# Expert selection of tokens 128 to 255 moved behind the places of the fetched tokens, and the first four row buffers put into the mixer's columns

## The chip, the cores and the metric

The kernel runs on one core of a Trainium2 chip. The core has five engines that run their own instruction streams in order and wait for each other through semaphores: TensorE (PE, matrix products; PEld is its weight load), VectorE (DVE), ScalarE (ACT), GpSimd (POOL) and SyncE (SP, which here only issues transfers). Transfers between HBM and the on-chip memory (SBUF) are carried out by 16 DMA engines, whoever issues them. The metric is the device time of one execution in microseconds (us). "Before" stands at a median of 1466.97 us over three runs, 1466.46 to 1468.75.

## The reference, cut to what matters

The model has two layers over 256 tokens of 1024 features. Layer 0 mixes the tokens by attention and retention, layer 1 by a short convolution; each is followed by the same channel mixer, PEER, which is where the change is:

```python
q  = (t @ w_q).reshape(n_tok, 8, 2, 128)              # 8 heads, two halves
sc = einsum('thpd,hpnd->thpn', q, sub_keys)           # 128 scores per head and half
s1, i1 = top_k(sc[:, :, 0], 16);  s2, i2 = top_k(sc[:, :, 1], 16)
top_s, pos = top_k(all sums s1 + s2, 16)              # 16 of 16 x 16 candidates
eidx = (i1 * 128 + i2) taken at pos;  gate = softmax(top_s)
hid  = gelu(einsum('td,thkd->thk', t, u[eidx]))
out  = einsum('thk,thkd->td', gate * hid, v[eidx])
```

Each token picks 8 x 16 = 128 of 16384 experts, and an expert is a row of `u` and a row of `v`.

## The kernel before

**Two ways to an expert.** The first 96 tokens (TG) fetch the rows of their own experts. One step of a class `Gather` is an indirect DMA on POOL's queue (line 997) that brings 128 rows of 1024 numbers (512 KB), one for each partition, and a DVE instruction that uses them: for `u` a product summed along the row (L1007), for `v` a scaled addition (L1018). A layer has 96 steps for `u` and 96 for `v`. The other 160 tokens (TD) go through all experts densely: TensorE multiplies them with each of 128 blocks of `u` (`dense_u`, L1400) and then of `v`, and the weights of the experts that a token did not pick are zero. The zeros and gates are laid out by 40 groups of four tokens (`onehots` on DVE, `g_mm` on TensorE, `g_put`).

**The stages of a PEER layer.** First the projection: for f = 0 to 15 TensorE computes the queries of one head half (`u_tile`, L302 with the high part of the weights, then L308 with the low part) and the scores of the half before (L1129, copied out by ACT at L1132). Then "u": a loop over i = 0 to 127, one block of `u` each. Then "v", likewise. The two parts of a projection weight come from `_split` (L177 on ACT for the high part, L179 for the low part, on POOL for all weights but f = 1 and 2); `u_tile(f)` writes the split of weight f + 2 into the program before it does its own products.

**What sets the order.** The order of the instructions of each engine is that of the program text. DVE's selection work is cut into pieces that stand in a queue `Pump`: each piece has a price, each turn of the loop adds credit (3.2 per f, 1.4 per i), and pieces are written out while the credit lasts. The pieces are: `stage1(th, f)` (the top 16 of the scores of one head half for token half th, that is tokens 0 to 127 or 128 to 255: five instructions, L1116 to L1124, shown as eight), and `chain(th, hf)` for four heads (`stage2_build`, L1146 to L1154; `stage2_top`, L1116 to L1124 on the candidates; `extract`, L1201 to L1223). `places(hf)` then makes the row numbers of the fetched tokens (L1255, L1256) and puts them into the tile `IG`, partly by three DMAs on POOL's queue (L1248), partly by a DVE copy (L1249). Only token half 0 holds fetched tokens. When the queue is empty, the groups start: `onehots`, and from then on DVE multiplies each block's result (L1443).

**Row buffers.** The fetched rows land in two buffers `grow` and four buffers in the tile `x2`, which is the mixer's and the projection's normalised input and is free once the projection's last high product has read it. `ga.widen()` takes over `x2` after the projection; `issue()` asks for rows as long as a buffer is free, the places are known (32 steps after `places(0)`, all 96 after `places(1)`) and `ga.open` is set, which happens at i == 2. Until then `grow` holds two blocks of `u` brought early (`PRE`, fetched by `fetch(i)` on SP's queue, L1104, among other spare places: `hg`, `uhi`, `ulo`, `xb`, `ko`, and the tile `one`, which with one `ulo` tile holds block 58). `ga.step()` writes a row's consumption into the program at a given rate per i; after each consumption `issue()` asks for the next row. The remaining blocks of `u` stream through a ring of eight tiles (`raw`, L153 on SP).

`extract` uses two scratch areas: M1 and M2 lie over the scores SC[0][0] and SC[1][0], whose selection has ended by then.

Of the kernel before, what the change touches and what calls it, by code (L numbers as in the profile page):

```python
# [12 lines left out]
F16 = mybir.dt.float16  # L13
# [214 lines left out]
def trunk_kernel(ctx, tc, x, xn, cst, mcst, ew_in, ew_out, ow_in, ow_out, wq, keys, pu, pe_, pv, pvn, pun, gains, out):  # L228
# [731 lines left out]
    class Gather:  # L960
# [8 lines left out]
        def __init__(self, pool):  # L969
            few = pool.tile([P, ROWS, D], F32, tag="grow", name=nm("grow"))  # L970
            self.rows = [few[:, i, :] for i in range(ROWS)]
            self.acc = [pool.tile([P, D], F32, tag=f"gacc{q}", name=nm("gacc")) for q in range(3)]
            self.hid = pool.tile([P, STEPS], F32, tag="ghid", name=nm("ghid"))
            self.known = 0
            self.open = False
            self.rate = 0.0
            self.i = 0
            self.c = 0
            self.credit = 0.0
            self.later = {}  # L980

        def widen(self):

            t = pers.tile([P, MORE, D], F32, tag="x2", name=nm("rows"))
            self.rows += [t[:, i, :] for i in range(MORE)]

        def row(self, s_):
            return self.rows[s_] if s_ < ROWS else self.rows[s_ % (ROWS + MORE)]

        def issue(self):  # L990

            while (self.open and self.i < self.TOTAL and (self.i < self.known or self.known == STEPS)
                   and self.i < self.c + len(self.rows)):
                s_ = self.i
                self.i += 1
                table = pun if s_ < STEPS else pvn
                gp.indirect_dma_start(self.row(s_), None, table,  # L997
                                      bass.IndirectOffsetOnAxis(IG[:, 0, s_ % STEPS:s_ % STEPS + 1].bitcast(U32), 0))
# [31 lines left out]
    def peer(l, before, norm):  # L1030
        with tc.tile_pool(name=nm("hg"), bufs=1) as hp:
# [14 lines left out]
            first_late = off[0] // TD  # L1046
            for s_ in SC:
                s_[0] = scr(hk)
            m1, m2 = SC[0][0], SC[1][0]

            def sc(th, f):
                o = f % PH * NK
# [53 lines left out]

            there = {}
            early = [i for i in sorted(PRE) if (PRE[i] < 14 or PRE[i] > 22) and i not in FIRST]
            early_u = [i for i in sorted(PRE) if 14 <= PRE[i] < 20]
            early_ko = [i for i in sorted(PRE) if 20 <= PRE[i] < 23]  # L1110
            pump = Pump()

# [21 lines left out]
            def stage1(th, f0, f1):  # L1134
                def g():
                    top16([(V[th][:, f * TK:(f + 1) * TK], IU[th][:, f * TK:(f + 1) * TK],
                            sc(th, f)) for f in range(f0, f1)])
                return g
# [33 lines left out]
                c = C[:, o:o + TK // 2].bitcast(F16).rearrange("p (a e) -> p a e", e=2)  # L1172
                return c[:, None].to_broadcast(by2)

            M1 = m1.bitcast(F16)[:, :HH * TK * TK]
            M2 = m2.rearrange("p (h k a) -> p h k a", h=HH, k=TK)
            N1 = M1.rearrange("p (n a e) -> p n a e", a=TK // 2, e=2)
            M1 = M1.rearrange("p (h k a) -> p h k a", h=HH, k=TK)
            N2 = m2.bitcast(F16)[:, :HH * TK * TK].rearrange("p (h k a) -> p h k a", h=HH, k=TK)

            def extract(th, hf):

                hs = slice(hf * HH, (hf + 1) * HH)
                ii = IF[th].rearrange("p (h s k) -> p h s k", h=PH, s=2)[:, hs]

                def of(t):
                    return t.rearrange("p (h k) -> p h k", h=PH)[:, hs]

                dd, b3 = of(dI[th]), of(bb)
                n = HH * TK
                pairs = [t[th][:, hf * 2 * n:(hf + 1) * 2 * n].rearrange("p (n e) -> p n e", e=2) for t in (PF, BP)]
                pf = pairs[0].rearrange("p (h k) e -> p h k e", h=HH)[:, :, :, 0]

                def wide(t):
                    return t[:, :, None, :].to_broadcast(by2)

                def f0():
                    src = PU[th].bitcast(U32)[:, hf * n:(hf + 1) * n]  # L1200
                    v.tensor_copy(pairs[0], src[:, :, None].to_broadcast([P, n, 2]))  # L1201
                    v.tensor_copy(dd[:, :, 0:1], ii[:, :, 0, 0:1])
                    v.tensor_tensor(dd[:, :, 1:], ii[:, :, 0, 1:], ii[:, :, 0, :TK - 1], OP.subtract)
                    v.scalar_tensor_tensor(dd, dd, CODE, C[:, None, C_DS:C_DS + TK].to_broadcast([P, HH, TK]),
                                           op0=OP.mult, op1=OP.add)

                def f1():
                    code = of(r1[th])
                    flat_code, flat_b = [t[:, hf * n:(hf + 1) * n, None].to_broadcast([P, n, 2]) for t in (r1[th], bb)]
                    v.tensor_tensor(b3, pf, code, OP.subtract)  # L1210
                    v.tensor_scalar(code, code, 1.0 / CODE, 1.0 / (2.0 * CODE) - 0.5, op0=OP.mult, op1=OP.add)
                    v.tensor_scalar(code, code, WHOLE, WHOLE, op0=OP.add, op1=OP.subtract)
                    v.scalar_tensor_tensor(pairs[1], flat_code, CODE, flat_b, op0=OP.mult, op1=OP.add)

                return [
                    (0.7, f0),
                    (1.2, lambda: v.tensor_tensor(N1, wide(pairs[0]), c4(C_ST), OP.is_ge)),
                    (1.2, lambda: v.tensor_tensor(M2, M1, dd[:, :, None, :].to_broadcast(n4), OP.mult)),
                    (1.2, lambda: v.tensor_reduce(of(r1[th]), M2, axis=AX.X, op=OP.add)),
                    (0.7, f1),  # L1220
                    (1.2, lambda: v.tensor_tensor(N1, wide(pairs[1]), c4(C_IB), OP.is_equal)),
                    (1.2, lambda: v.tensor_tensor(N2, M1, ii[:, :, 1:2, :].to_broadcast(n4), OP.mult)),
                    (1.2, lambda: v.tensor_reduce(of(r2[th]), N2, axis=AX.X, op=OP.add)),  # L1223
                ]
# [65 lines left out]
            for f in range(NPAIR):  # L1290
# [9 lines left out]
                if f:  # L1300
                    scores(f - 1)
                    pump.add((1.35, stage1(0, f - 1, f)))
                    if f <= HH * 2:
                        pump.add((1.35, stage1(1, f - 1, f)))
                    if f == HH * 2:
                        chain(0, 0)
                        pump.add((0.6, lambda: places(0)))
                    if early:
                        fetch(early.pop(0))
                pump.run(3.2)  # L1310
            ga.widen()
            ga.issue()

            def after_first():

                scores(NPAIR - 1)
                pump.add((1.35, stage1(0, NPAIR - 1, NPAIR)))
                chain(0, 1)
                pump.add((0.3, lambda: gates(0)), (0.6, lambda: places(1)))
                pump.add(*[(2.7, stage1(1, f, f + 2)) for f in range(HH * 2, NPAIR, 2)])  # L1320
                pump.add((0.0, lambda: gates_exp(0)))
                chain(1, 0)
                pump.add((0.6, lambda: gates_norm(0)), (0.3, shares))
# [99 lines left out]
            for i in range(NK):  # L1423
                ps = dense_u(i)
                if i == 2:
                    ga.open = True
                    ga.issue()
                if i == 0:
                    after_first()
# [204 lines left out]
```

## Time and profile before

| | |
|---|---|
| median of three runs | 1466.97 us |
| the profiled execution's own time | 1464.22 us |
| its span | 1462.5 us, mean granted clock 0.996 |
| busy, share of the span | PE 97%, PEld 91%, DVE 85%, ACT 54%, POOL 51% |
| moved by DMA | 532.84 MB, mean 364 GB/s |
| layer 1: first and last product of u start | 889.6 us, 1198.5 us |
| layer 0: first and last product of u start | 183.2 us, 491.3 us |

The span is cut from the first to the last instruction of the core; the execution's own time has 1.7 us more around it. Rows of the timeline give start, duration, engine, line, operation, output<-input, count, and in brackets how long the engine stood idle before it and what released it. Rows of the windows give a stretch, its length, the busy time and number of instructions of PE, PEld, DVE, ACT and POOL, the granted clock, the busy share of the DMA engines (1.02 is as full as it gets here) and GB/s.

### The profile page before, as it was taken

Reading aid. Unit: us, or ns where it says so; the run is one execution under the profiler, and the core shown is the slowest. Engines: PE = TensorE matmul, PEld = TensorE weight load, DVE = VectorE, ACT = ScalarE, POOL = GpSimd, SP = SyncE. Lnnn points to the kernel's source line nnn. Section 1 sums busy time; section 2 is a strip of 40 time slices with the busy share of each in tenths; the row PEclk is TensorE's granted clock in tenths of the full one; section 3 lists DMA queues with packets and bytes.
Section 4 is the critical chain, followed back from the end, with each engine's and each line's share of the span. In section 5 each row is a group of like instructions: output and inputs, shape, how many; then the busy total and the mean of one; then the engine's idle time right before and its main releaser. Section 6 shows DMA issues by size and latency. Waiting matters only on the chain.

```text
span 1462.5 us, 30103 instructions
## 1 busy us (share of the span) xinstructions
PE 1419.4 (97%) x11355; PEld 1336.2 (91%) x11364; DVE 1242.1 (85%) x2521; ACT 795.7 (54%) x1857; POOL 751.8 (51%) x505
## 2 busy tenths in 40 slices
PE   9999999999999999999999999999999999999997
PEld 5669999999998999989889999999999889988887
DVE  5628999968898799989987799997888879999997
ACT  6555422248776566666553452213887746665664
POOL 5753644546566346546145373454555535664650
PEclk9999999999999999999999999999999999999999
DMA  9546899999999999999976588999999999999994
GB/s 369 185 150 229 313 386 393 405 414 412 411 407 414 408 415 415 415 415 414 407 259 198 200 316 329 408 410 403 414 412 406 400 406 380 415 415 415 414 415 182
DMA packets 113875, 532.84 MB, mean 364 GB/s; under 512 B 13057, under 2 KB 13057, under 8 KB 84033
## 3 DMA queue, kind: packets, MB, share of 16 engines
q1 hardware_dynamic: 56448, 324.00, 56.5%
q0 software_dynamic: 56416, 204.29, 35.3%
q10 hardware_dynamic: 864, 2.62, 0.5%
q8 instruction: 89, 1.46, 0.4%
q14 instruction: 58, 0.47, 0.1%
HBM read 528.97 MB, written 1.05 MB: 362 GB/s over the span
## 4 chain that ended last, share of the span: by engine, by line
PE 41%; DMA 28%; DVE 14%; issue 10%; POOL 5%; ACT 1%; DVEq 0%; POOLq 0%; ACTq 0%
DMA rows<-pvn,ig 16%; PE hid L1400 13%; DMA rows<-pun,ig 6%; PE vo L1535 5%; PE hid L302 4%; POOL rows L997 4%; DMA grow<-pun,ig 3%; PE vo L1537 2%; PE vo L1501 2%; PE hid L308 2%; PE ea L334 2%; DMA grow<-pvn,ig 2%; PE ea L335 2%; DVE vlo L1418 2%; PE ea L336 2%
## 5 line engine op out<-in xcount | busy, mean ns | idle before, releaser
L1400 PE MATMUL hid<-xf,raw 128*128 128x160 f32 x3328 | 479.7, 301 | 11.8 <-DVE hg L1443 11.6
L1400 PEld LDWEIGHTS hid<-xf,raw 128*128 128x128 f32 x3328 | 458.2, 191 | 16.1 <-DVE hg L1443 16.0
L1411 ACT CAST vhi<-raw 128x1024 fp32r<-128x1024 f32 x222 | 229.5, 1048 | 183.8 <-DMA raw<-pv 111.9
L997 POOL DMA_INDIRECT rows<-pvn,ig x128 | 218.0, 1703 | 198.1 <-DVE gacc L1018 155.7
L1418 DVE TENSOR_TENSOR vlo<-raw,vhi 128x1024 bf16<-128x1024 f32 x222 | 266.5, 1218 | 17.2 <-ACT vhi L1411 16.7
L997 POOL DMA_INDIRECT rows<-pun,ig x128 | 152.4, 1190 | 127.3 <-DVE rows L1007 71.4
L1535 PE MATMUL vo<-ko,vhi 128*128 128x320 f32 x1200 | 213.3, 320 | 0.0
L179 POOL TENSOR_TENSOR lo<-raw,hi 128x1024 bf16<-128x1024 f32 x67 | 161.2, 2419 | 86.3 <-ACT hi L177 61.2
L1018 DVE SCALAR_TENSOR_TENSOR gacc<-rows,ghid,gacc 128x1024 f32<-128x1024 f32 x124 | 158.6, 1279 | 22.9 <-DMA rows<-pvn,ig 22.6
L1535 PEld LDWEIGHTS vo<-ko,vhi 128*128 128x128 f32 x1200 | 177.5, 189 | 0.0
L1537 PE MATMUL vo<-hb,vlo 128*128 128x160 bf16 x1776 | 162.0, 234 | 15.2 <-DVE vlo L1418 14.8
L1007 DVE SCALAR_TENSOR_TENSOR rows<-rows,xg 128x1024 f32<-128x1024 f32 x128 | 155.0, 1217 | 22.5 <-DMA rows<-pun,ig 22.1
L1440 ACT ACTIVATE hg<-hid 128x160 f32<-128x160 f32 (+14 forms) x240 | 62.7, 264 | 197.8 <-PE hid L1400 197.4
L1537 PEld LDWEIGHTS <-vlo 128*128 128x128 bf16 x1776 | 117.8, 98 | 42.8 <-DVE vlo L1418 23.3
L997 POOL DMA_INDIRECT grow<-pvn,ig x64 | 111.1, 1736 | 84.3 <-DVE gacc L1018 68.1
L1350 ACT ACTIVATE ko<-ko,idxT 128x128 f16<-128x128 f16 x320 | 101.7, 391 | 49.6 <-DVE ko L1335 49.3
L177 ACT CAST hi<-raw 128x1024 fp32r<-128x1024 f32 x100 | 103.1, 1050 | 30.4 <-PE hid L302 14.1
L997 POOL DMA_INDIRECT grow<-pun,ig x64 | 77.3, 1207 | 82.0 <-DVE grow L1007 44.9
L302 PE MATMUL hid<-x,hi 128*128 128x256 f32 x800 | 107.4, 287 | 3.3 <-DVE cg L934 2.7
L302 PEld LDWEIGHTS hid<-x,hi 128*128 128x128 f32 x800 | 98.5, 190 | 4.0 <-issue 2.9
L1535 PE MATMUL vo<-xf,vhi 128*128 128x320 f32 x576 | 102.1, 319 | 0.0
L1353 ACT ACTIVATE ko<-ko,idxT 128x128 f16<-128x128 f16 x320 | 101.1, 388 | 0.0
(251 smaller groups left out, 2240.3 us busy)
## 6 DMA issues: line engine op xcount, KB each, us to landing
raw<-pv SPq DMA_DIRECT2D x128, 1024.0 KB, 9.6
raw<-pu SPq DMA_DIRECT2D x104, 1024.0 KB, 8.1
raw<-wq SPq DMA_DIRECT2D x32, 512.0 KB, 4.2
raw<-ew_in SPq DMA_DIRECT2D x26, 512.0 KB, 6.8
raw<-ow_in SPq DMA_DIRECT2D x24, 512.0 KB, 5.7
hg<-pe_ SPq DMA_DIRECT2D x22, 512.0 KB, 6.3
raw<-ew_out SPq DMA_DIRECT2D x8, 512.0 KB, 3.3
raw<-ow_out SPq DMA_DIRECT2D x8, 512.0 KB, 3.8
```

The source lines that it names most:

```text
L177: self.nc.scalar.copy(hi, t)
L179: eng.tensor_tensor(lo, t, hi.bitcast(F32), OP.subtract)
L302: pe.matmul(ps[:, :S], hi[:, k * P:(k + 1) * P], A2[:, k, s_, :], start=k == 0 and s_ == 0, stop=False)
L997: gp.indirect_dma_start(self.row(s_), None, table, bass.IndirectOffsetOnAxis(IG[:, 0, s_ % STEPS:s_ % STEPS + 1].bitcast(U32), 0))
L1007: v.scalar_tensor_tensor(r, r, 1.0, XG[:, q % 2, :], op0=OP.mult, op1=OP.mult, accum_out=w)
L1018: v.scalar_tensor_tensor(self.acc[q], r, w, self.acc[q], op0=OP.mult, op1=OP.add)
L1350: act.activation(hi[:, j], lo[:, j], AF.Copy, scale=idxT[:, 1, t:t + 1])
L1400: pe.matmul(ps[:, :TD], w[k], xv["xf"][:, k, :], start=k == 0, stop=k == ND - 1)
L1411: act.copy(whi[j], raw)
L1418: v.tensor_tensor(wlo[j], raw, whi[j].bitcast(F32), OP.subtract)
L1535: pe.matmul(vo[b][:, TG:S + TD], hi[:, b * P:(b + 1) * P], hs, **m)
L1537: pe.matmul(vo[b][:, TG:S], lo[:, b * P:(b + 1) * P], hb, **m)
```

## The change

1. `stage1(1, f)` for f = 0 to 7 leaves the projection. All sixteen selections of token half 1 now stand in the queue behind `places(1)`, two at a time.
2. Since the scores SC[1][0] are now needed longer, the scratch of `extract` is moved: M2 to SC[0][0]; M1 to the tile `one` for token half 0 and to SC[1][0] for token half 1.
3. Block 58, which is brought into `one` and an `ulo` tile, is therefore no longer fetched at i = 0 but by a piece of price 0 in the queue behind `chain(0, 1)`.
4. The list of row buffers begins with the four of `x2`, then the two of `grow`. `ga.open` becomes a number: 4 right after the projection, all rows at i == 2 as before.

```diff
-            self.open = False
+            self.open = 0
...
-            self.rows += [t[:, i, :] for i in range(MORE)]
+            self.rows = [t[:, i, :] for i in range(MORE)] + self.rows
...
-            return self.rows[s_] if s_ < ROWS else self.rows[s_ % (ROWS + MORE)]
+            return self.rows[s_ % (ROWS + MORE)]
...
-            while (self.open and self.i < self.TOTAL and (self.i < self.known or self.known == STEPS)
+            while (self.i < min(self.open, self.TOTAL) and (self.i < self.known or self.known == STEPS)
...
-            m1, m2 = SC[0][0], SC[1][0]
+            m1, m2 = SC[1][0], SC[0][0]
...
-            early_u = [i for i in sorted(PRE) if 14 <= PRE[i] < 20]
+            early_u = [i for i in sorted(PRE) if 14 < PRE[i] < 20]
...
-            M1 = m1.bitcast(F16)[:, :HH * TK * TK]
+            M1s = [t.bitcast(F16)[:, :HH * TK * TK] for t in (one, m1)]
...
                     pump.add((1.35, stage1(0, f - 1, f)))
-                    if f <= HH * 2:
-                        pump.add((1.35, stage1(1, f - 1, f)))
                     if f == HH * 2:
                         chain(0, 0)
                         pump.add((0.6, lambda: places(0)))
...
+            assert ga.known
             ga.widen()
+            ga.open = MORE
             ga.issue()
...
                 chain(0, 1)
+                pump.add((0.0, lambda: fetch(58)))
                 pump.add((0.3, lambda: gates(0)), (0.6, lambda: places(1)))
-                pump.add(*[(2.7, stage1(1, f, f + 2)) for f in range(HH * 2, NPAIR, 2)])
+                pump.add(*[(2.7, stage1(1, f, f + 2)) for f in range(0, NPAIR, 2)])
...
                 if i == 2:
-                    ga.open = True
+                    ga.open = ga.TOTAL
                     ga.issue()
```

More of the change, by code (lines that the diff above doesn't have):

```diff
@@ L1173, in c4 @@
                 return c[:, None].to_broadcast(by2)
-            M1 = m1.bitcast(F16)[:, :HH * TK * TK]
+            M1s = [t.bitcast(F16)[:, :HH * TK * TK] for t in (one, m1)]
             M2 = m2.rearrange("p (h k a) -> p h k a", h=HH, k=TK)
-            N1 = M1.rearrange("p (n a e) -> p n a e", a=TK // 2, e=2)
-            M1 = M1.rearrange("p (h k a) -> p h k a", h=HH, k=TK)
             N2 = m2.bitcast(F16)[:, :HH * TK * TK].rearrange("p (h k a) -> p h k a", h=HH, k=TK)
             def extract(th, hf):
+                N1 = M1s[th].rearrange("p (n a e) -> p n a e", a=TK // 2, e=2)
+                M1 = M1s[th].rearrange("p (h k a) -> p h k a", h=HH, k=TK)
                 hs = slice(hf * HH, (hf + 1) * HH)
```

## The prediction

> **Where the time goes.** I read the page first: its busy shares and its slices say which engines can bind at all.
>
> ```profile
> PE 1419.4 (97%) x11355; PEld 1336.2 (91%) x11364; DVE 1242.1 (85%) x2521; ACT 795.7 (54%) x1857; POOL 751.8 (51%) x505
> ...
> DMA  9546899999999999999976588999999999999994
> ```
>
> TensorE is busy nearly everywhere, and the DMA engines are full through u and v of both layers; only around the mixers and projections do they have room. So an averaged share decides nothing, and the stage that the change touches has to be looked at: the end of a projection and the start of u. Next the chain of waits, over the end of layer 1's projection and all of its u:
>
> ```profile
> 886.52 1.90 PE hid L302 x16
> 888.42 0.89 PE hid L308 x8
> ...
> 892.38 119.53 PE hid L1400 x880
> ...
> 1057.00 11.80 DMA rows<-pun,ig
> ```
>
> In layer 1 TensorE itself is the chain through the last head half (high products, then from 888.42 the low ones, which need POOL's part of the weight) and through u up to the mid 1050s. One block costs 16 recorded products, 119.53 / 880 x 16 = 2.17 us. After 1057 the chain goes back and forth between row fetches and TensorE; grouped over that stretch:
>
> ```profile
> by line: PE hid L1400 26.2%; DMA rows<-pun,ig 23.4%; DMA rows<-pvn,ig 15.8%; issue 7.2%; DMA grow<-pvn,ig 6.3%; DMA raw<-pv 6.0%; PE G L1360 3.0%; ACT ko L1350 2.2%; ACT ko L1353 1.6%; POOL rows L997 1.4%; DVE rows L1007 1.1%; DVE hg L1443
> ```
>
> So u has two halves: first TensorE, then row fetches 45% to TensorE 29%. Windows show what each half has to spare (columns: busy us of PE, PEld, DVE, ACT, POOL, then clock, DMA share, GB/s):
>
> ```profile
> 885.00:890.00 5.00, 5.00 (x45) 4.78 (x44) 4.73 (x12) 1.39 (x6) 0.00 (x0) 1.00 0.87 326
> 890.00:895.00 5.00, 5.00 (x40) 5.00 (x39) 4.69 (x16) 2.55 (x7) 1.51 (x3) 1.00 1.02 406
> 895.00:900.00 5.00, 5.00 (x39) 5.00 (x38) 4.62 (x24) 0.61 (x2) 0.86 (x1) 1.00 0.84 318
> 900.00:905.00 5.00, 5.00 (x39) 5.00 (x39) 4.59 (x25) 0.61 (x2) 3.78 (x5) 1.00 0.67 215
> 905.00:910.00 5.00, 5.00 (x39) 5.00 (x38) 3.72 (x20) 0.81 (x3) 1.93 (x3) 1.00 1.01 347
> ```
>
> ```profile
> 985.00:1005.00 20.00, 20.00 (x150) 20.00 (x149) 16.45 (x32) 5.48 (x12) 13.34 (x10) 1.00 1.02 396
> 1005.00:1025.00 20.00, 20.00 (x155) 19.96 (x155) 12.31 (x22) 8.32 (x31) 6.91 (x9) 1.00 1.02 413
> 1125.00:1145.00 20.00, 17.96 (x146) 17.14 (x145) 16.20 (x29) 13.59 (x55) 10.15 (x9) 1.00 1.02 407
> 1145.00:1165.00 20.00, 18.39 (x157) 17.96 (x156) 17.38 (x25) 15.80 (x63) 13.04 (x10) 1.00 1.01 395
> 1165.00:1185.00 20.00, 17.33 (x140) 16.45 (x141) 17.06 (x27) 10.26 (x41) 9.54 (x9) 1.00 1.02 411
> ```
>
> The DMA engines' room at the start of u is, against 1.02, (0.15 + 0 + 0.18 + 0.35 + 0.01) x 5 / 1.02 = 3.4 us; that is all an earlier row fetch can fill. DVE idles 3.55 + 7.69 = 11.2 us from 985 to 1025. TensorE idles 2.04 + 1.61 + 2.67 = 6.3 us late in u, with the DMA engines full.
>
> **The moved selections and the port.** What happens at the seam is in POOL's and DVE's timelines:
>
> ```profile
> 868.57 2.37 POOL L179 TENSOR_TENSOR lo<-raw,hi 128x1024 bf16<-128x1024 f32 x1 [0.87 <-ACT hi L177]
> ...
> 875.05 2.38 POOL L179 TENSOR_TENSOR lo<-raw,hi 128x1024 bf16<-128x1024 f32 x1 [0.86 <-ACT hi L177]
> 878.29 2.37 POOL L179 TENSOR_TENSOR lo<-raw,hi 128x1024 bf16<-128x1024 f32 x1 [0.86 <-DMA hg<-pe_]
> 881.53 2.37 POOL L179 TENSOR_TENSOR lo<-raw,hi 128x1024 bf16<-128x1024 f32 x1 [0.87 <-ACT hi L177]
> 893.10 1.51 POOL L1248 DMA_DIRECT2D ig<-hg  x3 [9.20 <-DVE ig L1249]
> 899.13 1.01 POOL L997 DMA_INDIRECT grow<-pun,ig  x1 [4.52 <-DVE hg L1120]
> ```
>
> ```profile
> 848.46 2.28 DVE L545 TENSOR_TENSOR nw<-nw 128x2 f32<-128x2 f32 x1
> ...
> 874.98 0.28 DVE L1116 MAX8 hg<-hg 128x8 f32<-128x128 f32 x1
> ...
> 876.68 0.28 DVE L1116 MAX8 hg<-hg 128x8 f32<-128x128 f32 x1
> ...
> 878.39 2.36 DVE L1146 CAST hg<-hg 128x128 f16<-128x128 uint32 x1
> ...
> 881.61 0.33 DVE L1116 MAX8 hg<-hg 128x8 f32<-128x50 f32 x2
> ...
> 884.89 0.23 DVE L1201 CAST hg<-hg 128x128 f16<-128x128 uint32 x1
> ...
> 885.50 0.69 DVE L1217 TENSOR_TENSOR hg<-hg,cst 128x1024 f16<-128x1024 f16 x1
> 886.22 1.23 DVE L1218 TENSOR_TENSOR hg<-hg 128x1024 f32<-128x1024 f16 x1
> ...
> 892.84 0.18 DVE L1249 COPY ig<-hg 96x32 f32<-96x32 f32 x1
> ...
> 906.69 0.23 DVE L1146 CAST hg<-hg 128x128 f16<-128x128 uint32 x1
> ```
>
> One selection costs 876.68 - 874.98 = 1.70 us. Eight leave the projection, 13.6 us of DVE per layer, which on their own would put the places at 893.0 - 13.6 = 879.4. Two things stand against that. First, DVE then waits for scores: selection f = 7 of token half 0 can't begin before ACT has copied its scores,
>
> ```profile
> 867.11 0.43 ACT L1132 COPY hg<-sc 128x128 f32<-128x128 f32 x2
> ```
>
> so it runs 867.4 to 869.1. Second, the same cast L1146 takes 2.36 us at 878.39, under POOL's split, and 0.23 at 906.69; a product of two numbers a partition takes 2.28 at 848.46. [...] Before, one split falls on the chain of selection (881.53 runs under MAX8). Now the chain moves under the splits: the cast meets the one of 868.57 and ends by 871.0; the build ends 0.95 after POOL as before (881.61 - 880.66), at 871.9; the candidates' top 16 take 881.61 to 884.89, so to 875.2; the cast L1201 meets the split of 875.05, waits to 877.4; L1217 runs 877.9 to 878.6; the split of 878.29 waits for it, and L1218 for the split, to 881.0 instead of 886.2. The rest is unchanged: places at 893.0 - 5.2 = 887.8. Without the third meeting it would be 885.5, with none at all 883.3. I take 887.8, because L545 shows a two-input operation waiting out a whole split.
>
> [...]
>
> **The split queued behind the places.** Counting credit (3.2 per f; 1.35 a selection, 1.0 + 2.2 + 2.2 + 8.6 the chain, 0.6 the places), the turns f = 8 to 12 give 16.0. Before, 17.3 is needed (two selections, chain, places), so `places(0)` is written in turn 13. After, with one selection, 15.95 is needed: it is written in turn 12. But the split of the last weight, f = 15, is written at the start of turn 13. So on POOL's queue L1248, which waits for DVE, now stands ahead of that split instead of behind it. POOL issues at 887.8, is done at 889.4 (1.51), and splits until 889.4 + 2.37 = 891.7. TensorE wants this part at 888.42: it stalls **3.3 us** at the end of the projection (1.0 with places at 885.5, 0 with places at 883.3). Behind it wait its scores, block 0, and the transfers that wait for those products. Layer 0 has the same spacing, 11.57 us from last split to L1248:
>
> ```profile
> 175.11 2.37 POOL L179 TENSOR_TENSOR lo<-raw,hi 128x1024 bf16<-128x1024 f32 x1 [0.87 <-ACT hi L177]
> 186.68 1.50 POOL L1248 DMA_DIRECT2D ig<-hg  x3 [9.20 <-DVE ig L1249]
> ```
>
> **The earlier rows.** The first fetch follows the places' DMAs by 4.52 us (894.61 to 899.13), longer than the opening at i == 2 (889.76 + 2 x 2.17) takes; so not `ga.open` but the landing of the places binds. After: 889.4 + 4.5 = 893.9, 5.2 us earlier, and `x2` is free by then. Those four rows (2.1 MB, some 5 us at 406 GB/s) fill the room at 895 to 905. But the transfers of 889 to 893, which wait for TensorE's last products, come 3.3 us later and leave as much room there. I count zero: 3.4 us of room filled, some 3.3 opened. Ends: +1 us, and -3.4 us where TensorE does not stall.
>
> **Work moved into u.** 13.6 us of selections arrive in i = 14 to 28; DVE is 5.2 us ahead from the places; 8.4 us more lie against its 11.2 us of idle time at 985 to 1025. Hidden, with 2.8 us to spare; without that cover the groups of four tokens start later. By the credits they start at i = 65 instead of 58 anyway, and by then 51 rows instead of 56 are consumed; the 70 left to row 121 go at 1.37 instead of 1.28 per block. In time this is less:
>
> ```profile
> L1007 DVE SCALAR_TENSOR_TENSOR rows<-rows,xg x33: 1201/1218/1226, 912.9 to 1027.9; 128x1024 f32<-128x1024 f32 x33
> ...
> L1007 DVE SCALAR_TENSOR_TENSOR grow<-grow,xg x18: 1205/1218/1226, 907.7 to 1026.8; 128x1024 f32<-128x1024 f32 x18
> ```
>
> 51 rows in 120 us, 2.4 us a row whatever the program's rate: the fetches set the pace, and six buffers hold what comes while DVE waits. Cost 0; the upper end is the two rows that DVE may be short at i = 65, 4.8 us. The scratch in `one` changes no operation: 0. `fetch(58)` puts 512 KB behind the first rush, and SP waits at it for DVE:
>
> ```profile
> 901.10 28.58 SPq L153 DMA_DIRECT2D raw<-pu  x6
> ...
> raw<-pu SPq DMA_DIRECT2D x104, 1024.0 KB, 8.1
> ```
>
> The pair asked for at 901.10 is blocks 13 and 14, used from 889.8 + 0.5 + 13 x 2.17 = 918.5: 17 us ahead where 8.1 is needed. A wait of 3 us for DVE costs 0; over 9 us TensorE would wait for weights.
>
> **Sum.** A layer: 3.3 us at TensorE's last projection product, of which the 6.3 us of idle TensorE late in u may take back all or nothing. There the chain is 45% fetches, for which a late TensorE costs nothing, and 29% TensorE, so I take about half: 1.7 us a layer, **3.5 us** for both, ends 0 and 6.6. The profiled execution of 1464.22 (span 1462.5 and 1.7 around it) becomes 1467.7; the median lies 2.75 above that execution, so 1470.5.
>
> **Rivals.** (a) *The seam costs nothing net*: v and late u are bound by the bytes, TensorE's lateness is absorbed whole. For it: DMA 1.02 everywhere. Against: TensorE alone is the chain for the first 120 us of layer 1's u. 1467. (b) *The rows gain as meant*: POOL's splits don't collide as reckoned, L1248 starts before 888.42 - 2.37 - 1.51 = 884.5 (the point from which it decides), TensorE doesn't stall, fetches start as u begins, and part of the 3.4 us of DMA room is filled: some -2 a layer, 1463. For it: full DMA engines afterwards pass a head start on. Against: L1146. (c) *Groups too late*: nothing of the stall is taken back (6.6) and the denser second half of u adds 2 us a layer, beside DVE's 17 of 20 us busy there: 1477. For it: TensorE's idle time lies in just that stretch. It decides from the point where DVE is still at selections at i = 65. (d) That the rows are not earlier at all, as the landing of the places binds before and after, is part of (a).
>
> **Chances.** Forecast 0.34, (a) 0.28, (b) 0.20, (c) 0.18. The range reaches from (b) to (c), 1463 to 1477; the forecast's own is 1467 to 1474. Less than 0.2% (2.9 us) can't be told from no change: faster (below 1464.0) 0.18, from (b); same 0.36, from (a) and the low half of the forecast; slower 0.46.
>
> **What would show it.** Right: in POOL's timeline L1248 stands before the last L179, and the last L308 of the projection starts 3 us late after its L302; L1146 and L1201 take over 2 us; the first L997 is 5 us earlier against the fetch of before; the first group product comes 7 blocks later. Wrong: L179 ahead of L1248, or L1248 before 884, then TensorE's seam is gapless and (b) holds; or TensorE's idle time late in u shrinks by the whole stall, then (a); or DVE busy over 18 of 20 us from 1025 on with TensorE waiting for L1443, then (c).

## The result and the profile after

The changed kernel takes 1479.18 us in the median (1475.29 to 1485.39, six runs) against 1466.8 of the kernel before, measured with it: a ratio of 1.0083, 95% interval 1.0065 to 1.01, so slower by 9.5 to 14.7 us, 12.2 by the ratio. The forecast was 1470.5, its range ended at 1477. The direction and the mechanism at the seam came as written; the price was more than three times too small.

The profiled execution of after is the slowest of its six (1485.39 us, span 1483.6). Totals below are therefore taken from medians and ratios, and the trace is used for places and durations. Its first page has the same engine bound, with 21.1 us more span and 11.0 us more of busy TensorE, though the kernel has no product more (of the 11364 some records are missing in the page of before):

```profile
span 1483.6 us, 30076 instructions
...
PE 1430.4 (96%) x11364; PEld 1342.3 (90%) x11364; DVE 1243.8 (84%) x2507; ACT 793.4 (53%) x1843; POOL 754.5 (51%) x505
```

More busy time for the same products means that products take longer. The seam is one place where they do. First POOL's timeline of after, layer 0 and then layer 1, at the end of the projection:

```profile
171.91 2.51 POOL L179 TENSOR_TENSOR lo<-raw,hi 128x1024 bf16<-128x1024 f32 x1 [0.87 <-ACT hi L177]
181.16 1.51 POOL L1248 DMA_DIRECT2D ig<-hg  x3 [6.74 <-DVE ig L1249]
182.69 2.36 POOL L179 TENSOR_TENSOR lo<-raw,hi 128x1024 bf16<-128x1024 f32 x1
185.21 1.02 POOL L997 DMA_INDIRECT rows<-pun,ig  x1 [0.17 <-DVE hg L1118]
...
903.64 1.51 POOL L1248 DMA_DIRECT2D ig<-hg  x3 [6.74 <-DVE ig L1249]
905.16 2.36 POOL L179 TENSOR_TENSOR lo<-raw,hi 128x1024 bf16<-128x1024 f32 x1
```

L1248 stands ahead of the last split, as the credits said, and is issued at 181.16 where it was 186.68: 5.5 us earlier, forecast 5.2. The split waits behind it. TensorE's timeline at the same two places (brackets: idle before, and what ended it):

```profile
179.89 2.15 PE L302 MATMUL hid<-x,hi 128*128 128x256 f32 x16
185.10 1.89 PE L308 MATMUL hid<-xb,lo 128*128 128x256 bf16 x8 [3.06 <-POOL lo L179]
186.78 1.06 PE L1129 MATMUL sc<-ko,hg 128*128 128x128 f32 x4
187.63 3.96 PE L1401 MATMUL hid<-xf,hg 128*128 128x160 f32 x16
...
907.58 1.78 PE L308 MATMUL hid<-xb,lo 128*128 128x256 bf16 x8 [3.07 <-POOL lo L179]
909.15 1.06 PE L1129 MATMUL sc<-ko,hg 128*128 128x128 f32 x4
910.00 2.90 PE L1401 MATMUL hid<-xf,hg 128*128 128x160 f32 x16
```

The stall is 3.06 and 3.07 us, forecast 3.3. But the eight products of L308 then take 1.89 and 1.78 us, and the first block of u 3.96 and 2.90; in a kernel that does not stall there ("places back in turn 13" below) they take 1.05 and 2.34. The windows of after give the reason in the seventh number from the left, the granted clock (the first number is the length of the stretch):

```profile
185.00:192.00 7.00, 6.90 (x33) 6.47 (x34) 6.42 (x34) 0.81 (x3) 3.92 (x5) 0.58 0.81 316
192.00:199.00 7.00, 7.00 (x54) 7.00 (x53) 6.76 (x42) 2.93 (x7) 2.97 (x3) 1.00 1.03 415
907.00:914.00 7.00, 6.42 (x38) 6.04 (x39) 6.44 (x33) 1.33 (x6) 4.41 (x5) 0.76 0.76 281
914.00:921.00 7.00, 7.00 (x54) 7.00 (x53) 6.70 (x44) 2.41 (x5) 2.81 (x3) 1.00 1.03 414
```

In windows of 1 us the clock of after is 0.50 in each from 185 to 190 and from 908 to 911, and 1.00 at 191 and 912. A clock of 0.76 over 7 us is thus half speed for 2 x 0.24 x 7 = 3.4 us; 0.58 is 5.9 us of that window, and the stretch in layer 0 began before it: with 0.55 over 184 to 185 and 0.53 over 190 to 191 it is some 6.8 us. Half speed for 3.4 us loses 1.7 us of TensorE's work. This term is in no line of the prediction.

The selections, and what POOL's splits did to them, went as reckoned. DVE's timeline of after, layer 0:

```profile
162.88 1.77 DVE L1146 CAST hg<-hg 128x128 f16<-128x128 uint32 x1
...
168.79 2.33 DVE L1201 CAST hg<-hg 128x128 f16<-128x128 uint32 x1
...
171.50 0.69 DVE L1217 TENSOR_TENSOR one<-hg,cst 128x1024 f16<-128x1024 f16 x1
172.22 3.28 DVE L1218 TENSOR_TENSOR hg<-one,hg 128x1024 f32<-128x1024 f16 x1
```

Both casts meet a split (0.23 us without one) and end within 0.1 us of its end, and L1218 (1.23 us before) meets the third, which runs from 171.91 to 174.42.

How late TensorE is at each block of u tells where the rest of the time goes. The table is worked out from TensorE's timelines: the start of the first product of block i, less the same start in the kernel before, in us; the last column is the difference of the spans. Each row is one execution, good to 0.1 us, and two of one kernel differ by a few us (the first two rows); the execution of the kernel before is 2.75 us quicker than its median.

| kernel | layer 0: i=0 | 5 | 60 | 110 | 125 | layer 1: i=0 | 5 | 60 | 125 | end |
|---|---|---|---|---|---|---|---|---|---|---|
| after | 4.4 | 6.1 | 5.4 | 9.0 | 12.7 | 20.4 | 21.0 | 20.3 | 20.0 | 21.1 |
| after, run again | 3.4 | 4.4 | 3.8 | 5.8 | 7.9 | 15.0 | 15.4 | 14.8 | 15.3 | 16.2 |
| places in turn 13 | -0.1 | -0.1 | -0.8 | 0.6 | 2.4 | 4.1 | 4.1 | 3.4 | 8.3 | 10.9 |
| stall filled | 2.9 | 2.9 | 3.2 | 4.9 | 6.8 | 12.6 | 12.6 | 13.7 | 14.0 | 12.8 |
| seam alone | 9.4 | 10.5 | 10.5 | 12.2 | 11.1 | 23.6 | 24.4 | 24.4 | 24.8 | 26.9 |
| groups late alone | -0.2 | -0.2 | -0.9 | 2.5 | 4.5 | 5.5 | 5.5 | 4.8 | 5.3 | 5.0 |
| after, groups at 58 | 3.5 | 4.3 | 4.2 | 3.9 | 4.7 | 12.0 | 13.7 | 13.7 | 11.6 | 11.7 |
| 13, groups at 58 | -0.7 | -0.7 | -0.4 | -0.1 | 0.6 | 1.5 | 1.5 | 2.3 | 3.9 | 2.8 |
| 13, groups at 53 | -0.6 | -0.5 | 4.7 | 4.9 | 7.0 | 9.1 | 9.1 | 15.7 | 11.6 | 12.7 |

In after, what the seam costs is still there at i = 60 (5.4 of 6.1 us, 3.8 of 4.4) and is not taken back later; 4 to 7 us more are lost between i = 60 and 125 of layer 0. That is the stretch where the groups now begin: the first product of a group (L1361) starts within block 68, at 339.2, where it was within 61.

### The profile page after: what moved, and what is told of

Read it like the earlier page. It is cut to its first block, busy times and chain, and to the rows that moved or that the text cites. A ratio compares the mean times of both kernels' runs of the same rounds, so it can differ in the third digit from the quotient of the medians.

```text
span 1483.6 us, 30076 instructions
## 1 busy us (share of the span) xinstructions
PE 1430.4 (96%) x11364; PEld 1342.3 (90%) x11364; DVE 1243.8 (84%) x2507; ACT 793.4 (53%) x1843; POOL 754.5 (51%) x505
## 3 DMA queue, kind: packets, MB, share of 16 engines
HBM read 528.97 MB, written 1.05 MB: 357 GB/s over the span
## 4 chain that ended last, share of the span: by engine, by line
PE 56%; DMA 20%; DVE 13%; issue 6%; ACT 3%; POOL 2%; DVEq 0%; ACTq 0%; another core or an unknown queue 0%; POOLq 0%
PE hid L1401 24%; DMA grow<-pvn,ig 7%; PE vo L1536 7%; DMA rows<-pvn,ig 4%; PE hid L302 4%; DMA rows<-pun,ig 4%; PE vo L1538 4%; DVE vlo L1419 3%; PE vo L1502 3%; DVE gacc L1018 3%; DMA grow<-pun,ig 2%; PE hid L308 2%; DMA raw<-pv 2%; PE ea L334 2%; PE ea L335 2%
## 5 line engine op out<-in xcount | busy, mean ns | idle before, releaser
L1401 PEld LDWEIGHTS hid<-xf,raw 128*128 128x128 f32 x3328 | 459.0, 191 | 12.4 <-DVE hg L1444 12.2
L997 POOL DMA_INDIRECT rows<-pvn,ig x128 | 229.5, 1793 | 168.8 <-DVE gacc L1018 136.3
L1419 DVE TENSOR_TENSOR vlo<-raw,vhi 128x1024 bf16<-128x1024 f32 x222 | 266.0, 1217 | 18.1 <-ACT vhi L1412 17.9
L997 POOL DMA_INDIRECT rows<-pun,ig x128 | 149.2, 1166 | 150.0 <-DVE rows L1007 80.5
L1441 ACT ACTIVATE hg<-hid 128x160 f32<-128x160 f32 (+13 forms) x240 | 64.1, 269 | 226.8 <-PE hid L1401 197.3
L1538 PE MATMUL vo<-hb,vlo 128*128 128x160 bf16 x1776 | 161.4, 234 | 18.1 <-DVE vlo L1419 18.0
L1007 DVE SCALAR_TENSOR_TENSOR rows<-rows,xg 128x1024 f32<-128x1024 f32 x128 | 154.7, 1218 | 24.5 <-DMA rows<-pun,ig 23.9
L1018 DVE SCALAR_TENSOR_TENSOR gacc<-rows,ghid,gacc 128x1024 f32<-128x1024 f32 x124 | 158.5, 1278 | 16.3 <-DMA rows<-pvn,ig 12.2
L997 POOL DMA_INDIRECT grow<-pvn,ig x64 | 106.8, 1669 | 104.4 <-DVE gacc L1018 88.0
L302 PE MATMUL hid<-x,hi 128*128 128x256 f32 x800 | 109.4, 290 | 3.3 <-DVE cg L934 2.7
L302 PEld LDWEIGHTS hid<-x,hi 128*128 128x128 f32 x800 | 100.6, 194 | 4.1 <-issue 3.0
```

The lines of the kernel that those rows point to most:

```text
L302: pe.matmul(ps[:, :S], hi[:, k * P:(k + 1) * P], A2[:, k, s_, :], start=k == 0 and s_ == 0, stop=False)
L997: gp.indirect_dma_start(self.row(s_), None, table, bass.IndirectOffsetOnAxis(IG[:, 0, s_ % STEPS:s_ % STEPS + 1].bitcast(U32), 0))
L1007: v.scalar_tensor_tensor(r, r, 1.0, XG[:, q % 2, :], op0=OP.mult, op1=OP.mult, accum_out=w)
L1018: v.scalar_tensor_tensor(self.acc[q], r, w, self.acc[q], op0=OP.mult, op1=OP.add)
L1401: pe.matmul(ps[:, :TD], w[k], xv["xf"][:, k, :], start=k == 0, stop=k == ND - 1)
L1419: v.tensor_tensor(wlo[j], raw, whi[j].bitcast(F32), OP.subtract)
```

## The experiments

Ratios are against the kernel before on the same chip, with their 95% intervals.

**The changed kernel again.** Nothing is edited.

> The changed kernel itself, beside the variants of it and on the same chip. Both theories: some 12 us over the kernel before (1478 to 1481), with single executions several us apart, as the half-clock stretches differ in number from one execution to the next.

Measured: 1479.55 us (1474.16 to 1481.38), 1.0072 (1.0048 to 1.0096). The slowdown stands in a second set of runs.

**Places back in turn 13.** The change is kept; only the price of `places(0)` is raised so that it is written one turn later, behind the last split.

```diff
-                        pump.add((0.6, lambda: places(0)))
+                        pump.add((0.7, lambda: places(0)))
```

> The changed kernel with one price raised from 0.6 to 0.7, so that the places of the fetched tokens are written in turn 13, behind the split of the last projection weight; all else as changed. Theory S (the seam: the stalled low product of f = 15 and the half clock behind it, 6.1 us in layer 0 and 4.9 in layer 1, pass to the end whole): 1466 to 1469, no gap before the last L308, no half clock at the seam. Theory G (the later start of the groups of four tokens and the selections moved into u cost as much as the seam): 1472 to 1475 with no gap at the seam and TensorE's idle time late in u larger than before.

Measured: 1472.96 us (1468.48 to 1475.49), 1.0031 (1.0016 to 1.0046). POOL's and TensorE's timelines of this kernel:

```profile
175.03 2.59 POOL L179 TENSOR_TENSOR lo<-raw,hi 128x1024 bf16<-128x1024 f32 x1 [0.73 <-ACT hi L177]
181.85 1.50 POOL L1248 DMA_DIRECT2D ig<-hg  x3 [4.22 <-DVE ig L1249]
186.98 1.01 POOL L997 DMA_INDIRECT rows<-pun,ig  x1 [3.63 <-DVE hg L1124]
```

```profile
181.76 1.05 PE L308 MATMUL hid<-xb,lo 128*128 128x256 bf16 x8
...
183.09 2.34 PE L1401 MATMUL hid<-xf,hg 128*128 128x160 f32 x16
```

With the split ahead of L1248 neither the stall nor the half clock is there (1.05 and 2.34 us, as in the kernel before), and 1.0083 falls to 1.0031: some 7 us belong to the order on POOL's queue. The first fetch is still 5.8 us earlier than before (186.98 against 192.82; in the changed kernel it is 185.21, 7.6 us earlier), and 4.5 us of loss remain. So the seam is not all.

**The stall filled.** As the changed kernel, but 28 products into an unused accumulator stand between the high and the low products of f = 15, so that TensorE works while it would wait. What they compute is used by nothing.

```diff
+        if fill:
+            junk = acc_tile(3, nm("busy"))
+            for _ in range(fill):
+                pe.matmul(junk[:, :S], Ab[:, 0, :P], Ab[:, 0, :], start=True, stop=True)
...
-                ps = pair[f] if f < 2 else u_tile(xv["x2"], Xb)
+                ps = pair[f] if f < 2 else u_tile(xv["x2"], Xb, fill=28 if f == NPAIR - 1 else 0)
```

> The changed kernel with 28 products more (128x256, their result is not used) put between the high and the low products of f = 15, some 3.1 us, so that TensorE is not idle while it waits for the split. Theory S with the clock as a term of its own: the wait of 3.1 us stays, the half clock at the seam goes, 2.9 us less in layer 0 and 1.7 in layer 1: 4 to 5 us under the changed kernel. Rival (the clock drop costs nothing in the end, since late u takes it back): the same time as the changed kernel, within 1.5 us.

Measured: 1476.79 us (1475.67 to 1478.6), 1.0061 (1.004 to 1.0082). TensorE's timeline and the windows behind the seam:

```profile
179.52 2.15 PE L302 MATMUL hid<-x,hi 128*128 128x256 f32 x16
181.51 3.23 PE L310 MATMUL busy<-xb 128*128 128x256 bf16 x28
184.73 1.05 PE L312 MATMUL hid<-xb,lo 128*128 128x256 bf16 x8
...
186.06 2.34 PE L1405 MATMUL hid<-xf,hg 128*128 128x160 f32 x16
```

```profile
183.00:190.00 7.00, 7.00 (x58) 6.50 (x57) 6.41 (x35) 1.91 (x6) 5.53 (x5) 1.00 0.58 219
...
899.00:906.00 7.00, 7.00 (x59) 6.48 (x57) 6.42 (x34) 1.76 (x6) 5.70 (x5) 1.00 0.57 210
```

The clock stays at 1.00, where the changed kernel shows 0.58 and 0.76, when the same 3.2 us are worked through instead of idled: the half speed here comes from the idling, not from what the change computes. At i = 5 TensorE is 2.9 us late in place of 4.4 or 6.1. The gain of the whole kernel, 1.0083 (or 1.0072) to 1.0061, goes the same way but lies inside the intervals. The mean clocks of all executions go that way too: the span times one minus its mean granted clock, that is the time lost to the clock, is 10.8 us in the mean of either set of six runs of the changed kernel, 6.9 with the stall filled and 8.2 to 8.6 in the kernel before.

**The earlier rows alone.** The kernel before, with the new order of row buffers and `ga.open = MORE` after the projection; the selections stay where they were.

```diff
-            self.rows += [t[:, i, :] for i in range(MORE)]
+            self.rows = [t[:, i, :] for i in range(MORE)] + self.rows
...
             ga.widen()
+            ga.open = MORE
             ga.issue()
```

> The kernel before with the new order of the row buffers and four rows asked for right after the projection, nothing else (selections, scratch and block 58 as before). If the landing of the places is what binds the first fetch (as the prediction has it): 1467 within 1.5 us, first L997 at the same time as before within 1 us, only into another tile. Rival (asking earlier is a gain by itself): 2 us or more faster.

Measured: 1466.69 us, 0.9994 (0.9978 to 1.001). POOL's timeline of this kernel:

```profile
186.01 1.50 POOL L1248 DMA_DIRECT2D ig<-hg  x3 [9.19 <-DVE ig L1249]
192.25 1.02 POOL L997 DMA_INDIRECT rows<-pun,ig  x1 [4.73 <-DVE hg L1120]
```

The first fetch is at 192.25 (192.82 before): the landing of the places binds, not `ga.open`. By itself this half of the change neither costs nor gains. What rows are worth that really come earlier is not tested here, since here they don't.

**The seam alone.** The kernel before, with credit enough in turn 12 that `places(0)` is written there; all selections stay.

```diff
-                pump.run(3.2)
+                pump.run(4.6 if f == 12 else 3.2)
```

> The kernel before with 1.4 more credit in turn 12 alone, so that the places are written there, ahead of the last split on POOL's queue; the selections stay in the projection, rows as before. The places' DMAs then end at 894.6 as before and the split behind them at 897.0, where TensorE wants it at 888.4: 8.6 us of idle TensorE a layer, and half clock behind it. If such a loss passes whole to the end: 17 us and 3 to 6 of half clock, 1487 to 1490. If late u takes back half, as the prediction had it: 1476 to 1479.

Measured: 1487.21 us (1482.93 to 1491.21), 1.0129 (1.0106 to 1.0152), 18.9 us by the ratio. TensorE's and POOL's timelines:

```profile
190.10 1.89 PE L308 MATMUL hid<-xb,lo 128*128 128x256 bf16 x8 [8.62 <-POOL lo L179]
```

```profile
186.16 1.51 POOL L1248 DMA_DIRECT2D ig<-hg  x3 [12.44 <-DVE ig L1249]
187.69 2.36 POOL L179 TENSOR_TENSOR lo<-raw,hi 128x1024 bf16<-128x1024 f32 x1
```

With the places as late as before, the split behind them is later still: a stall of 8.62 us in each layer. The two stalls are 17.2 us, and the time goes up by 18.9. In the table 10.5 us at i = 5 of layer 0 are 11.1 at i = 125, and 24.4 of layer 1 are 24.8. This decides the step that I had settled by halves: in this execution u gives nothing back. (The extra credit also lets the groups begin one block earlier, in block 60.)

**The product with the gates later.** `shares`, which the extra selections push from i = 33 to 40 by the credits, brings the gates; DVE's product L1014 waits for them (5.9 and 6.1 us in after, no such wait before). Here it is written 12 steps behind the last of the first 32 rows in place of 4, once on top of "places in turn 13" and once on the changed kernel.

```diff
-                    self.later[s_ + 4] = lambda: v.tensor_tensor(w, w, g, OP.mult)
+                    self.later[s_ + (12 if q == 0 else 4)] = lambda: v.tensor_tensor(w, w, g, OP.mult)
```

> The changed kernel with the places in turn 13 (price 0.7) and the product of the first 32 steps' sums with their gates (L1014) written 12 instead of 4 rows after the last of them, when the gates' DMA has long landed. With the places in turn 13 alone it stood 4.6 to 6 us over before. Theory W (DVE's wait of 6.1 to 6.8 us a layer for that DMA, with rows landed and not used, is what is left): 1466 to 1468.5, no wait at L1014. Theory G (the groups' start at i = 65 is what is left): 1471 to 1474, the wait gone and the time not.

> The changed kernel with only the gates' product written 8 rows later; the places stay in turn 12, so the seam stalls as in the changed kernel. Theory W: the seam's share alone is left, 6 to 8 us over before (1473 to 1475). Theory G: as the changed kernel, 1478 to 1480.

Measured: 1472.57 us, 1.0042 (1.0026 to 1.0058), and 1482.36 us, 1.0106 (1.0088 to 1.0123). The wait is gone in both and no time is gained. DVE's waits in layer 0 of "places in turn 13", and then of the kernel without that wait (line, what it waited for: total, times, longest):

```profile
DVE ghid L1014 <- DMA ig<-hg: 6.8, 1, 6.8
...
DVE g L1279 <- ACT idxT L1277: 5.4, 1, 5.4
```

```profile
DVE g L1279 <- ACT idxT L1277: 10.4, 1, 10.4
```

DVE reaches L1279, the copy ahead of the groups, 5 us earlier and waits 5 us longer there: TensorE's transposes for it stand at a fixed block. The six microseconds at L1014 were time that DVE had to lose.

**The groups earlier.** The same kernel with more credit a step of u, so that the groups start at i = 58 again in place of 65.

```diff
-                        pump.run(1.4)
+                        pump.run(1.57)
```

> The kernel of e5_gates_later with 1.57 instead of 1.4 credit a block, so that by the credits the groups start at i = 58 as before. Theory W: no better than e5_gates_later, within 1.5 us. Theory G: 1465 to 1468 and 3 us or more under e5_gates_later, the late half of u with no more idle TensorE than before.

Measured: 1466.57 us (1462.96 to 1470.54), 0.9997 (0.9986 to 1.0009). Six microseconds came back, and with them all that was left. It is the whole change without its two side effects, and it equals the kernel before although its rows start 5 to 6 us earlier: in the timelines DVE uses row 0 of layer 0 at 195.9 (201.2 before), row 24 at 258.2 (259.5), row 60 at 342.9 (341.9). The head start is used up in the stretch in which DVE now has the eight selections to do; that these use it up is an argument, no run has the one without the other.

**The groups late alone.** The kernel before with less credit a step of u: the groups start at i = 65, nothing else is moved.

```diff
-                        pump.run(1.4)
+                        pump.run(1.2)
```

> The kernel before with one number changed: each step of u hands the queue of small jobs 1.2 credits in place of 1.4. By the credits worked through by hand the groups of part 2 then start at i = 65 in place of 58, as in the changed kernel, and the shares of tokens 0 to 127 are asked for at i = 38 in place of 33; nothing else is moved, the seam is as before, and DVE has no selection more in u. Theory G (the groups' late start costs by itself, since TensorE's transposes come late and rows that have landed are left standing): 5 to 6 us over the kernel before, 1472 to 1473. Rival (it costs only together with the eight selections that the change moved into u, which make DVE late for the same work): within 2 us of before, 1465 to 1469.

Measured: 1469.89 us (1467.47 to 1474.64), 1.0023 (1.0008 to 1.0037): 1.2 to 5.4 us, between the two expectations. With the groups all that stands behind the same credits comes later, the gates of `shares` too (a wait of 2.5 and 2.1 us at L1014). Windows of the kernel before and then of this one, where the groups begin in layer 0:

```profile
300.00:365.00 65.00, 65.00 (x538) 64.51 (x537) 49.35 (x104) 47.30 (x177) 35.30 (x29) 1.00 1.02 413
```

```profile
300.00:365.00 65.00, 65.00 (x525) 64.62 (x525) 41.84 (x86) 40.40 (x146) 30.59 (x26) 1.00 0.98 389
```

From 300 to 365 DVE does 7.5 us less, and the DMA engines bring 65 x (413 - 389) GB/s = 1.56 MB less, 3.8 us at 413 GB/s: rows are in, DVE stands before L1279 (10.9 us, 3.7 in the kernel before), and fetches wait for buffers. That this is the loss is not shown: TensorE's waits for DVE's product L1443, where it would be missed, are 5.0 and 2.6 us in the two layers (4.6 and 7.0 before), and both kernels have one stretch of 3.4 us at half clock in u of layer 0 (0.98 over 365 to 445 in the kernel before, 0.96 over 445 to 492 in this one).

The time goes at the groups themselves. In all kernels the last of the 40 groups stands in block 119, so a later start packs them closer: 51 blocks in place of 58. TensorE's timeline at one group of the kernel before and at one of this kernel:

```profile
332.99 0.61 PE L1360 MATMUL G<-ko 128*128 128x128 f16 x8
```

```profile
425.40 0.22 PE L1360 MATMUL G<-ko 128*128 128x128 f16 x1
426.24 1.11 PE L1360 MATMUL G<-ko 128*128 128x128 f16 x7 [0.61 <-ACT ko L1353]
```

The products need what ACT scales in L1350 and L1353 (2.3 us a group). The view of L1360 lists what the loads of their weights waited for, over both layers of this kernel; in the kernel before that list is empty:

```profile
  ACT ko L1353: 10.0, 37
  ACT ko L1350: 1.0, 2
```

Counted from each of the 320 group products to the next product on TensorE, the groups of layer 0 take 24.4 us (18.1 before) and those of layer 1 21.8 (17.9), while the products of u between i = 60 and 125, counted alike, take no longer (150.6 and 149.1 us; 152.1 and 153.2 before), so a part is had back there. All seven profiled executions with the groups in block 68, two of the changed kernel among them, show 21.1 to 24.4 us a layer and 9 to 13 us of such waits; the seven with the groups in block 61 or earlier show 17.9 to 19.7 and at most 2.7. This is read from traces; no run starts the groups late and keeps their spacing.

**The changed kernel with the groups at 58.**

```diff
-                        pump.run(1.4)
+                        pump.run(1.57)
```

> The changed kernel with 1.57 credits a step of u in place of 1.4, so that the groups start at i = 58, where they start before; the seam stays as the change made it (the split behind the places, the stall of 3.06 us and the half clock behind it in both layers). If seam and late groups are two separate terms (7 to 8 and 5 to 6 us): 1473.5 to 1475, about 5 us under the changed kernel. Rival (the late groups cost nothing behind a seam that has already made u late, and the whole 12.4 us is the seam): 1478 to 1481. Rival (the seam's loss is taken back once the groups are early): 1467 to 1469.

Measured: 1475.19 us (1473.52 to 1475.95), 1.0049 (1.0032 to 1.0066), 7.2 us by the ratio. The two terms are separate: with the seam alone left 7.2 us (the rival of a cost of 0 behind a late seam falls, that of a seam taken back too), with the groups alone left 4.5 (places in turn 13); 7.2 + 4.5 = 11.7 against the 12.2 of the whole change.

**Earlier than 58.** On the kernel of "the groups earlier", 1.7 credits (groups at 53); and on the kernel before, 1.5 (groups at 52).

```diff
-                        pump.run(1.57)
+                        pump.run(1.7)
```

```diff
-                        pump.run(1.4)
+                        pump.run(1.5)
```

> The kernel of the experiment with the groups earlier (change kept, places priced so that they are written in turn 13, gates' product later), with 1.7 credits a step of u in place of 1.57: the groups start at i = 53 in place of 58. Theory G carried on (each step of delay costs about 0.8 us): 4 us under it, 1462 to 1464, under both kernels. Rival (from i = 58 on the groups are no longer what u waits for; DVE's selections are, which only get crowded): no change or slower, 1466 to 1470.

> The kernel before with 1.5 credits a step of u in place of 1.4: the groups start at i = 52 in place of 58, shares at i = 29 in place of 33; nothing else. Theory G carried on (about 0.8 us a step): 1462 to 1463. Rival (58 is early enough, the kernel before waits for its rows or for DVE): within 1.5 us of before, 1465.5 to 1468.

Measured: 1473.66 us, 1.0043 (1.0024 to 1.0063), and 1468.83 us, 1.0015 (1.0002 to 1.0028). The line "each step of delay costs 0.8 us", carried on to the other side, falls: earlier is slower too, so of the starts tried 58 is the best on both. TensorE's waits for ACT in layer 0 of the first of the two, both of them in its timeline, and ACT's row between them:

```profile
PE hid L1401 <- ACT hg L1441: 3.3, 2, 2.3
```

```profile
282.07 2.44 PE L1401 MATMUL hid<-xf,hg 128*128 128x160 f32 x16 [1.01 <-ACT hg L1441]
...
293.32 2.44 PE L1401 MATMUL hid<-xf,raw 128*128 128x160 f32 x16 [2.29 <-ACT hg L1441]
```

```profile
291.25 0.40 ACT L1234 ACTIVATE hg<-hg,nw 128x128 f32<-128x128 f32 x1 [7.35 <-DVE hg L1230]
```

The wait for ACT at 282 and 293 is new, and in the table 5 us are lost by i = 60 in layer 0 and 6.6 in layer 1; a part of it is the first groups, which here stand ahead of i = 60. What keeps ACT is in its row: it stands 7.35 us before L1234, a step of the gates that waits for DVE's selections (14.7 us over both layers; 7.8 with the groups at 58), and the results of the blocks (L1441) stand behind it in ACT's program.

No version beat the kernel before.

## Why the prediction missed, step by step

- **"The moved selections and the port": right.** Both casts and L1218 took longer beside splits (L1146 1.77 us, where over 2 was forecast, L1201 2.33, L1218 3.28), and the places came 5.5 us earlier where 5.2 was written. "The port" is my name for this; no run shows what the two engines share. Nor does a row of the kernel before show that a split waits for L1217, as the sum has it; in after the third split, which begins 0.28 us before L1217 ends, took 2.51 us where the three ahead of it took 2.37. Not every operation with two inputs takes longer: L728 takes 0.69 us in all eight places, at 62.54 of after inside two splits that run from 61.47 to 66.20.
- **"The split queued behind the places": right in place and size, and one term short.** The turn, the order on POOL and the stall (3.06, 3.07 against 3.3) are as written. What the stall does to TensorE's clock was not priced: 3.4 us at half speed or twice that behind it, 1.7 to 3.4 us lost in each layer. At i = 5 TensorE was 4.4 to 6.1 us late for a stall of 3.06. The two speeds are in the rows, 1.05 and 1.89 us for the same eight products, and in the clock, 1.00 and 0.50; the stretch at 0.50 lasts some 6.8 us in layer 0 and 3.4 in layer 1.
- **"The earlier rows": that the landing of the places binds is right** (the earlier rows alone, 192.25 against 192.82), though the fetch came sooner after L1248 than reckoned (186.98 - 183.35 = 3.6 us, not 4.5). The net 0 is borne out only together with the moved selections: with the groups at 58 and no stall, rows 5 to 6 us earlier leave 0.9997.
- **"Work moved into u": the step that failed by most, beside the sum.** The eight selections are hidden, as written: with the groups at 58 the time is that of before. But the groups' later start was set to 0 with the argument that "the fetches set the pace". It costs 1.2 to 5.4 us alone and 4.5 in the changed kernel, both layers together, where the upper end of 4.8 stood for one layer. The argument was a misreading. The same view of L1007, over 885 to 1028, lists what DVE waited for ahead of its row steps, and then who waited for these steps:

```profile
  DMA rows<-pun,ig: 5.7, 7
  DMA grow<-pun,ig: 3.9, 4
...
  POOL rows L997: 24.5, 16
  POOL grow L997: 20.3, 12
```

  In these 120 us DVE waited 9.6 us for rows, and the fetches 44.8 us for DVE: the 2.4 us a row are mostly the pace of DVE's program. The step had looked for DVE being short of time when the groups start; the traces show TensorE waiting for ACT at groups that are packed closer. That `shares` moves too, and a wait of 6 us with it, was overlooked; it cost nothing.
- **"Sum": wrong.** "I take about half" was a middle between two ends, not a reading. TensorE is 98% busy in u, as the window of layer 0 of the kernel before shows,

```profile
180.00:490.00 310.00, 305.26 (x2397) 301.45 (x2397) 267.19 (x695) 156.96 (x571) 164.83 (x138) 0.99 1.01 404
```

  and idle time in u is not by itself time to catch up: in the seam alone TensorE comes 10.5 us late and its waits for L1443 in layer 0 are 5.4 us where they were 4.6, so 10.5 us were passed on as 11.1. Nothing taken back, 6.6 us, was in the text as an end; measured is 7.2 with the half clock in it.
- **The rivals.** (c), groups too late with nothing taken back, 1477, had both terms and came nearest, but by DVE at selections in place of TensorE waiting for ACT; it had a chance of 0.18 and set the range's end. (a) and (b) fall: nothing was absorbed, and TensorE stalls.

What stays open is how the seam's 7.2 us divide: stall and half clock add up to 9.5 to 13 us over both layers in the traces, so 2 us or more come back somewhere (in layer 1 of "after, groups at 58" 13.7 us at i = 60 are 11.6 at i = 125), and the spread of two executions of one kernel is as large. That the half clock by itself costs the whole time something is shown at i = 5, and only pointed at by the totals.

## What to carry to other kernels

A piece of work that is moved takes its place on every queue that it issues on: here 1.5 us of transfers on POOL moved ahead of one split that TensorE waits for, and cost 7 us. Price a stall of the bound engine with what it does to that engine's clock (here 3.06 us of idle time were followed by 3.4 to 6.8 us at 0.50), and let nothing be taken back unless a row shows where that engine would otherwise have idled. When the credits of a planner are spent on moved work, look at what starts later by it, and retune the rate with the change: 1.57 in place of 1.4 was worth 5 of the 12 us. Look for the loss at the moved work itself first: packed closer, it can outrun what feeds it, here ACT.

## What the runs showed of the hardware

**Idle times of TensorE and the clock behind them.** For the 14 profiled executions of this study I put each idle time of TensorE of 0.7 us or more beside the mean granted clock of the 7 us behind it, and counted those under 0.95:

| idle time | followed by a slower clock |
|---|---|
| under 1.7 us | 4 of 173 |
| 1.7 to 2.3 us | 14 of 38 |
| 2.3 to 2.9 us | 21 of 32 |
| 2.9 us and more | 18 of 19 |

So between 1.7 and 2.9 us, where 35 of 70 were followed by a slower clock, the idle time alone does not decide, and the same place differs between executions. The four under 1.7 us lie where TensorE waited twice within 2 us (0.38 and 0.93 us at 1139 and 1140 of "groups late alone"). In the timeline of after, one wait late in u and the one ahead of layer 1:

```profile
428.89 1.60 PE L1401 MATMUL hid<-xf,raw 128*128 128x160 f32 x8 [2.93 <-DVE hg L1444]
...
782.07 3.75 PE L302 MATMUL hid<-x,hi 128*128 128x256 f32 x16 [2.70 <-DVE cg L934]
```

The sixteen products of L302 at 782.07 take 3.75 us where 2.15 is usual, and the clock is 0.50 over 785 to 787; in the kernel before, at 768.80, they take 2.14 us after an idle time of 2.69, at a clock of 1.00 over 769 to 776. The spread between runs of one kernel, which is 10 us here, is only in part this: over the 172 executions with a clock on record, each taken against the mean of its kernel, the time lost to the clock and the whole time correlate at 0.49, so the clock goes with about a quarter of the variance. From the table I estimate that seven waits of 1 us, if they lie apart, cost less clock than two of 3.5; no run tries it.

**A DVE operation that waits out a split shows as a long one.** L1218 takes 3.28 us beside a split and 1.23 without, with no idle time in front of it: in the groups the 2.05 us more count as busy time.
